# One projection of an attention block as seven products of 2x2 blocks instead of four plain ones

## The chip, the core and the metric

The kernel runs on one core of a Trainium2 chip. The metric is device time in microseconds (us) of one execution, lower is better; the time of a version is the median of several runs. The core has five engines that work side by side and wait for each other by semaphores: PE (TensorE, matmuls, whose weight loads the profile shows apart as PEld), DVE (VectorE), ACT (ScalarE), POOL (GpSimd) and SP (SyncE, used here to issue DMAs). DMAs are issued on the queues of SP, ACT and POOL. Matmuls write to PSUM, eight banks of 128 x 512 floats, which DVE and ACT empty into SBUF.

## The reference

A decoder layer over 512 tokens of 1024 channels, in float32. `h = rms_norm(x)`, then one projection gives the inputs of two attention branches of 8 heads of 64 channels each:

```python
proj = h @ w_in[l]
qa, ka, va, za, qb, kb, vb, zb, gl_a, gl_b = jnp.split(proj, SPLIT_POINTS, axis=-1)
...
oa = moba_attention(qa, ka, split_heads(va, N_HEADS_MOBA), rel_bias)
ob = stick_breaking_attention(split_heads(qb, N_HEADS_SB), split_heads(kb, N_HEADS_SB),
                              split_heads(vb, N_HEADS_SB))
ya = (merge_heads(oa) * jax.nn.silu(za)) @ w_up_moba[l]
yb = (merge_heads(ob) * jax.nn.silu(zb)) @ w_up_sb[l]
y = jax.nn.sigmoid(gl_a + gb[:D_MODEL]) * ya + jax.nn.sigmoid(gl_b + gb[D_MODEL:]) * yb
x = x + y @ w_out[l]
```

The first branch is causal softmax attention with normed q and k and a bias. The second takes `z = q k / 8` and weights each value by sigmoid(z) times the product of the (1 - sigmoid(z)) of the keys between. The change concerns `qb`, 512 tokens by 512 channels.

## The kernel before

**Precision.** Every float32 operand is split into a high part, rounded to the format that PE multiplies, and a low part, the rest. `mm3` (lines 214 to 219) makes one product of three matmuls: high by low, low by high, high by high, added up in PSUM.

**The weights' stream.** All weights lie in one array `w` of blocks of 128 x 1024 floats (512 KB), in the order in which they are used; `_layout` builds it on the host from `FRONT` and `FILLS` (lines 46 to 55). `load_w` (143) hands out the next block and keeps three under way. `fetch_w` (150) brings a block: a DMA on SP's queue into one of three raw tiles (line 162), the high part on ACT (line 171), the low part on DVE (line 173), each into one of three tiles. Blocks that are sums of others skip the DMA on SP: they have been put together in a tile of pool `vp` (eight tiles of 128 x 1024, which also hold the transposed q and k of the first branch for a while and the finished values) by a DMA that loads one block and a DMA that adds another (`accum_op`), both on POOL's queue. `load_v` (107) and `add_v` (114) do that for the values, `sum_w` (130) for the output projection.

**Order.** Tile, the layer under the kernel, orders the instructions of each engine when the program is built and assigns buffers then. `tc.issue_after(ins)` puts an instruction behind another on the same engine.

1. Norm of x, q and k of the first branch, then seven merge gates (`FRONT`).
2. `values()` (644 to 683): va and vb as seven products of 2x2 blocks (the scheme of Strassen in the variant of Winograd). x^T is cut into four blocks of 512 channels by 256 tokens, w likewise. Four sums of blocks of x^T (S1 to S4) are made by `mix_x` (345), four of blocks of w (T1 to T4) by the adding DMAs. `product` (635) multiplies one block of x^T (as PE's weights) by one block of w (128 x 512 moving): 24 matmuls of 128x512 on two weight blocks. The products are added up on the way out of PSUM (lines 657 to 682).
3. Eight pairs of heads, four of each branch (774 to 793). A pair is: `scores` (485), 24 matmuls into six banks with tag `s`; the weighted sum of the pair before the last (`finish`, 768, with `weighted`, 577), into a bank with tag `pj`, emptied by DVE at line 591; then for each head softmax (510) or stick-breaking (526), 32x32 transposes (554), a way through DRAM and back (`put` on SP's queue, `get` on ACT's). PE does not wait for that: `fill()` (756) puts projections between, from the list `FILLS`, one entry of it at each of four places per pair. The entries are `z`, the gates `g`, `q` and `k` of the second branch, and `up`, two products of the branch's output with its up matrix. Each is one block of the weights' stream.

A projection is `chunk_ct` (476): one block of 1024 columns holds the weights of 128 channels; 8 x 3 matmuls with 128x128 of the weights as PE's weights and 128 channels by 512 tokens of x^T moving give 128 channels by 512 tokens in one bank, with tag `pj` (two banks) or `s`. `f_q` (602) scales that by 1/8 and splits it with `split` (401) for `scores`; q has four such entries.

4. The rest of the second branch's up products, and the output projection as seven products of the same kind.

## Time and profile before

| | |
|---|---|
| time, median of 3 runs | 385.66 us (385.57 to 385.77) |
| the profiled execution | 385.91 us, of it 384.1 span of the core |
| matmuls | 1863 |
| DMAs with weights on SP's queue (512 KB) | 58, median 5.4 us from issue to landing |
| DMA packets | 35882, 83.22 MB, 217 GB/s in the mean |

The profile is that of one execution, so sums are made against its 385.91 us. "Busy" of PE counts each matmul from its start to its modelled end, in a pipeline: 389 ns for a matmul of 128x512, though the next one starts earlier. What a matmul costs is therefore read from the distance of starts, which the chain in order of time gives. In rows of groups stands the line, engine, operation, out<-in, shape, count, then busy time in us and mean ns of one, then the idle time of the engine before them and what ended it. In rows of a timeline stand the start and the length in us. Times within the kernel count from the start of the span.

### The profile page before, as it was taken

The numbers are of one execution on the slowest core, as the hardware profiler recorded it, in microseconds if no ns is written. First come the engines' busy times: TensorE is split into PE (matmuls) and PEld (weight loads), VectorE is DVE, ScalarE is ACT, GpSimd is POOL, SyncE is SP. The second block draws the span as 40 slices with busy tenths as digits, with TensorE's granted clock in tenths as the row PEclk, the third lists the DMA queues.
The fourth block names the chain that finished last, engine by engine and source line by source line (L and its number), as shares of the span: only waits on it lengthen the run. The fifth ranks groups of instructions, "written<-read, shape, count | busy, mean of one in ns | idle before, by whom it ended". The sixth has DMA issues, their size and how long they took to land.

```text
span 384.1 us, 5319 instructions
## 1 busy us (share of the span) xinstructions
PE 379.7 (99%) x1863; PEld 306.5 (80%) x1863; DVE 283.3 (74%) x495; ACT 204.4 (53%) x345; POOL 74.7 (19%) x117
## 2 busy tenths in 40 slices
PE   8999999999999999999999999999999999999996
PEld 5888888888888888878787887887878877888885
DVE  4828999934786868696775948939849725999963
ACT  5775657347755747774665428327245222368540
POOL 3859959220100000000000000002000000330310
PEclk9999999999999999999999999999999999999999
DMA  7989798996710567886766485894876851599955
GB/s 272 330 333 336 211 214 287 267 332 216 162 58 3 190 192 254 250 275 163 263 148 232 127 292 188 194 342 135 203 280 185 263 208 56 148 266 297 164 148 181
DMA packets 35882, 83.22 MB, mean 217 GB/s; under 512 B 3848, under 2 KB 16648, under 8 KB 35856
## 3 DMA queue, kind: packets, MB, share of 16 engines
q1 hardware_dynamic: 27840, 53.24, 42.0%
q0 software_dynamic: 5568, 18.90, 20.5%
q10 hardware_dynamic: 2448, 10.75, 8.1%
q8 instruction: 14, 0.23, 0.2%
q14 instruction: 12, 0.10, 0.1%
HBM read 65.03 MB, written 14.70 MB: 208 GB/s over the span
## 4 chain that ended last, share of the span: by engine, by line
PE 99%; DVE 0%; issue 0%
PE gl L217 8%; PE gl L218 8%; PE gl L219 8%; PE poa L586 2%; PE pob L586 2%; PE sa L496 2%; PE sb L496 2%; PE zb L217 2%; PE kb L217 2%; PE qb L217 2%; PE yb L217 2%; PE za L217 2%; PE yb L218 2%; PE ka L218 2%; PE ka L217 2%; PE qb L218 2%
## 5 line engine op out<-in xcount | busy, mean ns | idle before, releaser
L173 DVE TENSOR_TENSOR wl<-wr,wh 128x1024 fp32r<-128x1024 f32 (+1 forms) x62 | 73.2, 1181 | 41.4 <-ACT wh L171 41.3
L171 ACT ACTIVATE wh<-wr 128x1024 fp32r<-128x1024 f32 (+1 forms) x62 | 63.8, 1029 | 42.7 <-PE ya L219 10.8
L217 PE MATMUL gl<-xl,wh 128*128 128x512 f32 x128 | 49.8, 389 | 0.0
L218 PE MATMUL gl<-xh,wl 128*128 128x512 f32 x128 | 49.8, 389 | 0.0
L219 PE MATMUL gl<-xh,wh 128*128 128x512 f32 x128 | 49.8, 389 | 0.0
L132 POOL COPY turn_of<-ptb 1x1 f32<-1x1 f32 x3 | 1.5, 504 | 174.4 <-DMA ptb<-pdb 174.4
L613 ACT ACTIVATE gl<-gl,x 128x512 f32<-128x512 f32 x16 | 11.0, 686 | 37.4 <-PE gl L219 32.9
L219 PEld LDWEIGHTS gl<-xh,wh 128*128 128x128 f32 x128 | 24.0, 188 | 5.0
L217 PEld LDWEIGHTS gl<-xl,wh 128*128 128x128 f32 x128 | 24.0, 188 | 5.0
L218 PEld LDWEIGHTS gl<-xh,wl 128*128 128x128 f32 x128 | 24.0, 188 | 5.0
L516 DVE CUSTOM_DVE_ANT_0 pa<-sa,om 128x512 f32<-128x512 f32 (+3 forms) x32 | 14.2, 482 | 11.0 <-PE sa L496 11.0
L536 DVE TENSOR_TENSOR_SCAN sx<-om,begin 128x512 f32<-128x512 f32 (+1 forms) x16 | 17.0, 1075 | 4.5 <-ACT om L533 4.5
L518 ACT ACTIVATE pa<-pa,m 128x512 f32<-128x512 f32 (+3 forms) x32 | 17.7, 554 | 4.0 <-DVE m L516 3.9
L558 DVE STREAM_TRANSPOSE turnedb<-pb 128x384 f32<-128x384 f32 (+1 forms) x24 | 14.1, 600 | 0.0
L558 DVE STREAM_TRANSPOSE turneda<-pa 128x384 f32<-128x384 f32 (+1 forms) x24 | 14.1, 604 | 0.0
L217 PE MATMUL zb<-xl,wh 128*128 128x512 f32 x32 | 12.8, 400 | 0.0
L217 PE MATMUL kb<-xl,wh 128*128 128x512 f32 x32 | 12.7, 396 | 0.0
L217 PE MATMUL qb<-xl,wh 128*128 128x512 f32 x32 | 12.7, 396 | 0.0
L217 PE MATMUL yb<-olb,wh 128*128 128x512 f32 x32 | 12.6, 393 | 0.0
L217 PE MATMUL za<-xl,wh 128*128 128x512 f32 x32 | 12.6, 393 | 0.0
L218 PE MATMUL zb<-xh,wl 128*128 128x512 f32 x32 | 12.5, 390 | 0.0
L218 PE MATMUL yb<-ohb,wl 128*128 128x512 f32 x32 | 12.5, 390 | 0.0
(385 smaller groups left out, 1022.9 us busy)
## 6 DMA issues: line engine op xcount, KB each, us to landing
wr<-in_w SPq DMA_DIRECT2D x58, 512.0 KB, 5.4
pda<-turneda SPq DMA_DIRECT2D x32, 160.0 KB, 2.9
pta<-pda ACTq DMA_DIRECT2D x8, 640.0 KB, 5.5
pdb<-turnedb SPq DMA_DIRECT2D x32, 160.0 KB, 4.2
ptb<-pdb ACTq DMA_DIRECT2D x8, 640.0 KB, 6.4
xn<-in_x SPq DMA_DIRECT2D x8, 256.0 KB, 6.0
om<-e_dr SPq DMA_DIRECT2D x8, 256.0 KB, 4.7
xr<-in_xT SPq DMA_DIRECT2D x7, 256.0 KB, 5.6
```

The source lines that it names most:

```text
L171: A.activation(hi[:, a:b], raw[:, a:b], AF.Copy)
L173: low[c] = V.tensor_tensor(lo[:, a:b], raw[:, a:b], hi[:, a:b].bitcast(F32), op=ALU.subtract).ins
L217: T.matmul(ps, aH, bL, start=start, stop=False, skip_group_check=on)
L218: T.matmul(ps, aL, bH, start=False, stop=False, skip_group_check=on)
L219: end[0] = T.matmul(ps, aH, bH, start=False, stop=stop, skip_group_check=on).ins
L496: T.matmul(ps[b][:, c:c + n], x[o, i * P:(i + 1) * P], y[o, :n], start=m == 0, stop=m == 2)
L516: V.tensor_tensor_reduce(rows[i], sc[i], bias[:, S - n:], scale=1.0, scalar=3e38, op0=ALU.add, op1=ALU.min, accum_out=m[:, 0, i:i + 1])
L518: A.activation(rows[i], rows[i], AF.Exp, bias=m[:, 0, i:i + 1], scale=-1.0, accum_out=m[:, 1, i:i + 1])
L536: V.tensor_tensor_scan(sx[:, n - 1::-1] if n == S else sx[:, :n][:, ::-1], om[:, S + 1 - n:][:, ::-1], begin[:, S - n:S][:, ::-1], 0.0, op ...
L558: V.transpose(turned[:, :, at:at + n, :].rearrange("p q j r -> p j q r"), rows[i].rearrange("p (j q c) -> p j q c", j=n, q=4))
L586: guard[0] = T.matmul(po[o, :].rearrange("p (a n r) -> p a n r", a=4, r=32)[:, :, i:i + n, :], vv[j][:, c:c + HD], src, start=j == NT - 1, ...
L613: evicted.append(A.activation(g, ps, AF.Sigmoid, bias=mb[:, i:i + 1]).ins)
```

## The change

qb is computed as seven products as well, right behind the values, by `queries()`. There the blocks of w are PE's weights and those of x^T move, so that the result stands in columns (channels by tokens) as `scores` wants it. `product_ct` is such a product: on one weight block, for n of two halves of 128 channels and k of four blocks of 128 input channels, one `mm3` with 128x128 of w and 128 x 256 tokens of x^T, so 24 matmuls of 128x256. The blocks and sums of x^T are those that the values use. The sums of w's blocks are made by the same pair of DMAs on POOL's queue, four of them (T1 to T4), each one tile of 512 KB. Results go to two tiles of pool `vp`; `f_q` then only scales and splits, from SBUF, and takes no weight block.

`FILLS` loses the four weight blocks of q. Its entries per pair hold two blocks in the first pair, three in the second to seventh and four in the eighth (before: three in the first four, four in the others); one more stands behind the pairs in both. The up products take both banks with tag `s` wherever they stand.

```diff
-FILLS = ("q:0", "k:0", "za:0", "",
-         "za:1", "q:1", "g:7", "",
-         "k:1", "za:2", "g:8", "",
-         "q:2", "za:3", "g:9", "",
-         "k:2", "q:3", "zb:0", "g:10",
-         "zb:1", "k:3", "up:0", "g:11",
-         "zb:2", "g:12", "up:1", "g:13",
-         "zb:3", "g:14", "up:2", "up:3",
+FILLS = ("za:0", "k:0 q:0", "", "",
+         "za:1", "g:7 q:1", "k:1", "",
+         "za:2", "g:8", "zb:0", "",
+         "za:3", "k:2 q:2", "g:9", "",
+         "zb:1", "g:10", "k:3 q:3", "",
+         "zb:2", "g:11", "up:0", "",
+         "zb:3", "g:12", "up:1", "",
+         "g:13", "g:14", "up:2", "up:3",
          "g:15")
...
+    ORDER = {"v": ("11", "22", "T2", "21", "T3", "T1", "T4"), "q": ("11", "T1", "21", "T2", "22", "T3", "T4")}
...
     def f_q(p):
-        qb.append(split(chunk_ct(f"qb{p}"), f"qb{p}", HD ** -0.5))
+        qb.append(split(q_raw[p // 2][:, p % 2, :], f"qb{p}", HD ** -0.5))
...
         for t in range(2):
             A.activation(low_b[t], X[t], AF.Copy)
+        summed.append(each(add_sum, "q", ("T1",), each(load_sum, "q", ("T1",), summed[-1])))
         Y = [bank("s", f"vw{t}") for t in range(2)]
         product(Y, s1, True)
...
+        summed.append(each(add_sum, "q", ("T2",), each(load_sum, "q", ("T2",), summed[-1])))
         product(X, a22, False)
...
+    def product_ct(ps, a, start):
+        hi, lo = load_w()
+        for n in range(2):
+            for k in range(4):
+                ks = slice((2 * k + n) * P, (2 * k + n + 1) * P)
+                mm3(ps[:, n * HS:(n + 1) * HS], hi[:, ks], lo[:, ks], *a[k], start and n + k == 0, k == 3, True)
+
+    def queries():
+        q = [wide(f"qb{c}").rearrange("p (n t) -> p n t", n=2) for c in range(2)]
+        q11, q21, q12, q22 = (q[c][:, :, r * HS:(r + 1) * HS] for c in range(2) for r in range(2))
...
+        X, D, Z, Y, E = (bank("s", f"q{n}") for n in "xdzye")
+        product_ct(X, a11, True)
+        A.activation(q11, cols(X), AF.Copy)
+        product_ct(D, s1, True)
+        A.activation(q22, cols(D), AF.Copy)
+        summed.append(each(add_sum, "q", ("T3",), each(load_sum, "q", ("T3",), summed[-1])))
+        product_ct(Z, a12, True)
+        V.tensor_tensor(q11, cols(Z), q11, op=ALU.add)
+        product_ct(X, s2, False)
+        V.tensor_tensor(q12, q22, cols(X), op=ALU.subtract)
+        each(add_sum, "q", ("T4",), summed[-1])
+        product_ct(Y, s4, True)
+        V.tensor_tensor(q12, cols(Y), q12, op=ALU.add)
+        product_ct(X, s3, False)
+        V.tensor_tensor(q22, q22, cols(X), op=ALU.subtract)
+        A.activation(q21, cols(X), AF.Copy)
+        product_ct(E, a22, True)
+        V.tensor_tensor(q21, cols(E), q21, op=ALU.add)
+        return q
+
+    q_raw = queries()
...
         for kind, i in fills.pop(0):
+            home[0] = "s" if kind == "up" else tag
             make[kind](i)
```

`load_sum` and `add_sum` are `load_v` and `add_v` with the kind (values or q) as an argument. On the host, `_layout` cuts the columns of q into four blocks ahead of the fills instead of four blocks of 128 channels among them; the bytes are the same.

## The prediction, made before the result was known

> **What bounds the kernel now.** I read the page first (busy time, then the chain that ended last), the chain in order of time, the busy time of each engine by stage, and last the single instructions of DVE, POOL and PE where the change lies. The page and the head of its chain:

> ```profile
> span 384.1 us, 5319 instructions
> ...
> PE 379.7 (99%) x1863; PEld 306.5 (80%) x1863; DVE 283.3 (74%) x495; ACT 204.4 (53%) x345; POOL 74.7 (19%) x117
> ...
> PE 99%; DVE 0%; issue 0%
> ```

> TensorE is never let go: what is taken from its work comes off the time, as long as nobody makes it wait. The chain in order of time gives the starts of the eight pairs of heads:

> ```profile
> 126.03 2.07 PE sa L496 x24
> ...
> 144.63 2.07 PE sa L496 x24
> ...
> 163.23 2.07 PE sa L496 x24
> ...
> 184.15 2.07 PE sa L496 x24
> ...
> 205.07 2.07 PE sb L496 x24
> ...
> 231.43 2.07 PE sb L496 x24
> ...
> 257.79 2.07 PE sb L496 x24
> ...
> 284.15 2.07 PE sb L496 x24
> ```

> A pair is its scores (2.07), from the third pair on the weighted sum of two pairs before, and its projections. The stages, with length and busy time of PE, PEld, DVE, ACT, POOL, then clock, DMA share and GB/s:

> ```profile
> 57.00:88.00 31.00, 31.00 (x138) 25.68 (x137) 21.63 (x40) 14.73 (x22) 14.05 (x16) 1.00 0.97 301
> 88.00:126.00 38.00, 38.00 (x170) 31.20 (x168) 26.53 (x30) 24.93 (x33) 1.79 (x2) 1.00 0.37 106
> 126.03:144.63 18.60, 18.60 (x98) 15.30 (x98) 13.97 (x39) 11.79 (x24) 0.00 (x0) 1.00 0.62 185
> ...
> 184.15:205.07 20.92, 20.92 (x118) 16.57 (x118) 15.19 (x41) 12.41 (x25) 0.00 (x0) 1.00 0.69 222
> 205.07:231.43 26.36, 26.36 (x142) 21.08 (x142) 18.68 (x27) 12.24 (x21) 0.00 (x0) 1.00 0.60 205
> 231.43:257.79 26.36, 26.36 (x142) 21.07 (x142) 21.43 (x29) 11.66 (x20) 1.60 (x3) 1.00 0.76 227
> ```

> PE fills every stage, even the one from 57 to 88 us in which the DMA engines are busy 0.97 of the time.

> **The change, part by part.** *Removed:* four projections of q, 24 matmuls of 128x512 each. A pair with four projections lasts 26.36, one with three 20.92: a projection costs 5.44 us of PE, and four cost 21.8. The values confirm the step: 168 matmuls of 128x512 are their 7 products, in 38.0 us, 0.226 us each.

> *Added:* seven products of 2 x 4 x 3 = 24 matmuls, 168 in all, each with 256 moving columns and a fresh 128x128 block of weights. The trace has that form in the last product, in the chain in order of time:

> ```profile
> 376.44 0.12 PE ox L217
> ...
> 377.88 0.23 PE ox L217
> ...
> 379.26 0.12 PE ox L217
> ```

> Between the first two rows lie 12 matmuls of 128x256: 1.44 us, 0.120 each. Between the last two, 6 of 128x512: 1.38 us, 0.230, slower than the 0.226 of the values. Scaled by 0.226/0.230 the step is 0.118, which I take: 168 of them are 19.8 us. The bounds are 0.120 (20.2) and half of 0.226 (19.0). So PE has 21.8 - 19.8 = 1.9 us less to do (rounded from 21.76 and 19.82), between 1.6 and 2.8.

> For the weights, this is the row of a load:

> ```profile
> L218 PEld LDWEIGHTS qb<-xh,wl 128*128 128x128 f32 x32 | 6.0, 188 | 1.2
> ...
> L217 PEld LDWEIGHTS ox<-wl,yh 128*128 128x128 f32 x16 | 3.0, 189 | 0.5
> ```

> A load takes 188 ns from start to end, the matmuls of the last product follow each other at 120: loads overlap the matmuls and each other there, so 72 more loads cost nothing beyond the step. [...]

> *Weight splits.* Seven blocks of 1024 columns in place of four: three more times ACT L171 and DVE L173. The products also empty PSUM with three copies and six sums where q had none; the split of each q head pair stays, now from SBUF.

> ```profile
> L173 DVE TENSOR_TENSOR wl<-wr,wh 128x1024 fp32r<-128x1024 f32 (+1 forms) x62 | 73.2, 1181 | 41.4 <-ACT wh L171 41.3
> L171 ACT ACTIVATE wh<-wr 128x1024 fp32r<-128x1024 f32 (+1 forms) x62 | 63.8, 1029 | 42.7 <-PE ya L219 10.8
> ```

> and from the groups of the values' stage:

> ```profile
> L668 DVE TENSOR_TENSOR vas<-vz,vas 128x512 f32<-128x512 f32 x2 | 1.4, 686 | 0.6 <-PE vz L219 0.6
> ...
> L673 ACT ACTIVATE vc<-vx 128x512 f32<-128x512 f32 x2 | 1.2, 598 | 1.1 <-PE vx L219 1.1
> ```

> In the 19.8 us of the new stage DVE has 7 x 1.18 + 6 x 0.69 = 12.4, ACT 7 x 1.03 + 3 x 0.60 = 9.0. A block lasts PE 24 x 0.118 = 2.83 us there and 38.0/14 = 2.71 in the values, which run without a gap at the same work per block. I cost it at nothing; the cover is 7 us of free DVE.

> *The sums of q's blocks* (three loads and four adding DMAs of 512 KB on POOL's queue) stand behind v's last adding DMA. Each waits for the one it builds on, and POOL waits with it; nothing else is on POOL until the fifth pair. ACT waits for a sum at its split, and behind that wait stand the splits of the next blocks and the copies out of PSUM, so a late sum stops PE.

> ```profile
> 99.01 0.90 POOL L121 DMA_DIRECT2D vT2b<-in_w  x1 [0.84 <-DVE wl L173]
> ...
> 105.40 1.23 DVE L173 TENSOR_TENSOR wl<-vT3a,wh 128x1024 fp32r<-128x1024 f32 x1
> ...
> 111.33 1.22 DVE L173 TENSOR_TENSOR wl<-vT1a,wh 128x1024 fp32r<-128x1024 f32 x1
> ```

> ```profile
> DMA to landing us min/median/max: 5.7/8.7/12.2
> ```

> ```profile
> DMA to landing us min/median/max: 5.1/7.3/10.0
> ```

> The last two rows are v's loads (L112) and v's adding DMAs (L121). Of the eight tiles of that pool six hold v's sums at 100 us and one the values' first half, so one is free: I start the first load at 99.9. With median landings (8.7, 7.3): T1 is loaded at 108.6 and summed at 115.9; T2's load takes the tile that T3a leaves at 106.6, is issued at 109.5 and lands at 118.2, its sum at 125.5; T3 lands at 127.8, its sum at 135.1. The blocks come on PE at 126.0 + 2.83 n: T1 at 128.9, T2 at 134.5, T3 at 140.2, T4 at 143.0. A split needs 2.2 us before that: 126.7, 132.3, 138.0, 140.8. T4 is added into T2's tile after T2's split, which starts when PE leaves the third block before it, at 128.9, and ends at 131.1; it lands at 138.4. The margins are 10.8, 6.8, 2.9 and 2.4 us: no wait.

> *The pairs.* They hold two projections in the first, three in the next six and four in the last. The first lasts 2.07 + 2 x 5.5 = 13 us. The next pair's scores need the banks of its scores, last read here 9.1 us after the start of the pair:

> ```profile
> 134.86 0.28 DVE L516 CUSTOM_DVE_ANT_0 pa<-sa,om 128x128 f32<-128x128 f32 x1
> ```

> That leaves 4 us. The pairs of the second branch fall from 26.36 to 20.9. The fifth keeps three weight splits and the evictions of z, k and q, 18.7 us of DVE (its row above); the sixth loses two splits and one eviction of k, 21.4 - 2 x 1.18 - 0.68 = 18.4. DVE is then busy nine tenths of the pair, ACT under two thirds. The DMA share rises to at most 0.76 x 26.36 / 20.92 = 0.96 with nothing taken off, the share at which the stage from 57 us kept PE full. The tight place is the bank of the weighted sum, which the second projection of a pair takes over:

> ```profile
> 209.38 0.50 PE L217 MATMUL kb<-xl,wh 128*128 128x512 f32 x1
> ...
> 213.78 0.68 DVE L591 TENSOR_TENSOR oa<-poa,za 128x512 f32<-128x512 f32 x1
> ...
> 214.95 0.39 PE L217 MATMUL qb<-xl,wh 128*128 128x512 f32 x1
> ...
> 239.76 0.68 DVE L591 TENSOR_TENSOR oa<-poa,za 128x512 f32<-128x512 f32 x1
> ...
> 265.59 0.68 DVE L591 TENSOR_TENSOR ob<-pob,zb 128x512 f32<-128x512 f32 x1
> ...
> 292.41 0.68 DVE L591 TENSOR_TENSOR ob<-pob,zb 128x512 f32<-128x512 f32 x1
> ```

> L591 frees it 0.5 us before the second projection in the fifth pair; at the same 9.9 us after the start the margin is 0.9 in the sixth, 1.4 in the seventh and 0.9 in the eighth. I leave it at nothing, since before L591 DVE has the same stick-breaking work as now. The up products move into the scores' banks, straight ahead of the next scores in the sixth and seventh pair: their second eviction (0.69, the form of L668) has until the third group of scores, two thirds into the 2.07, so 0.7 us to spare; nothing too.

> The sum against the profiled execution: 385.91 - 1.9 = 384.0, its span 384.1 - 1.9 = 382.2. The median of the runs is 385.66, 0.25 below that execution, so the forecast is 383.8, with a range of its own from 383.0 (2.7 off) to 384.5 (0.7 of stalls).

> **The rivals.** *A, the late bank.* One weight split more ahead of L591 (1.2 us) in the fifth to eighth pair makes PE wait 0.7, 0.3, 0 and 0.3. That is 1.3: 385.1. For it: the 0.5 us of margin and DVE at nine tenths. Against: there are fewer splits per pair.

> *B, the sums come late, and the kernel is slower.* If the free tile goes to another use, the first load waits for T3a's tile at 106.6, 6.7 us later, and T3's sum passes its 2.9 us of margin by 3.8: PE waits 3.8, the net is +1.9, 387.6. It decides from a start at 102.8 on; every us beyond costs one, and from 104.7 the gain is gone. The longest landings (12.2 and 10.0) would do the same from 99.9. Against it: in this stage the DMA share is 0.37, and the two adding DMAs issued in it at 97.3 and 99.0 landed in 5.1 and 5.9, below the medians I used:

> ```profile
> vT2a<-in_w POOLq DMA_DIRECT2D x1, 512.0 KB, 5.1
> vT2b<-in_w POOLq DMA_DIRECT2D x1, 512.0 KB, 5.9
> ```

> *C, weight loads not hidden:* 72 more at 188 ns are 13.5, less 1.9: 397.3. For it speaks only that a load is longer than the step of 128x256; the 24 matmuls of the last product speak against it.

> **How the numbers follow.** A measurement of this kernel can tell about 0.2%, 0.8 us: faster is below 384.9, slower above 386.4. Forecast 0.66; A 0.17, of which a third falls below 384.9; B 0.14; C 0.03. So faster is 0.66 + 0.05 = 0.71, the same 0.12, slower 0.17. The range goes from the forecast's lower bound, 383.0, over A to 386.0, where a second split stands ahead of L591 in one of those pairs (0.9 more); B and C, 0.17, are left out.

> **What would show it.** Right: the new stage of 168 matmuls lasts 19.8 us at 0.118 each without a gap; the pairs start 13.0, 18.6 and then 20.9 apart; PE's share stays at 99%; ACT's splits of q's four sums wait for PE, not for a DMA. Wrong: a step near 0.13 or more, which takes all of the gain; ACT or POOL waiting for the sums of T2, T3 or T4 with a gap on PE behind it; a gap of PE ahead of the second projection of a pair or of the scores, ended by DVE L591 or L711; pairs of 22 us and more, which would make DVE the bound there.

## The result, and the profile after

The changed kernel takes 389.1 us (median of 6 runs, 387.68 to 389.66), the kernel before 385.7 (6 runs beside them, 385.54 to 385.98): a ratio of 1.0084, with a 95% interval of 1.0067 to 1.0100. The forecast was 383.8, with a range of 383.0 to 386.0. It was wrong, and on the wrong side. The profiled execution of the changed kernel took 388.84 us, 387.1 of it span. The ratios, here and below, leave out an execution more than 1.5% above the fastest of its kernel; that is one, the slowest of kernel 1 below.

The page of the changed kernel, its span, PE's busy time and the chain that ended last by engine:

```profile
span 387.1 us, 5491 instructions
...
PE 379.2 (98%) x1935; PEld 309.3 (80%) x1935; DVE 290.3 (75%) x503; ACT 209.0 (54%) x351; POOL 79.4 (21%) x124
...
PE 95%; DVE 2%; DMA 1%; issue 1%; ACT 0%; DVEq 0%; ACTq 0%
```

PE held 99% of the chain before; now it waits somewhere. The starts of the eight pairs in the chain in order of time show where:

```profile
145.53 2.05 PE sa L504 x24
...
158.68 2.07 PE sa L504 x24
...
177.28 2.07 PE sa L504 x24
...
198.20 2.07 PE sa L504 x24
...
219.12 0.91 PE sb L504 x5
...
245.19 2.07 PE sb L504 x24
...
266.11 2.07 PE sb L504 x24
...
287.02 2.07 PE sb L504 x24
```

The pairs last 13.15, 18.6, 20.92, 20.92, **26.07**, 20.92 and 20.91. All but the fifth are as forecast. Stretches of the changed kernel (length, busy time of PE, PEld, DVE, ACT, POOL, then clock, DMA share, GB/s): the stage of q with the last matmul of the values and the step to the scores, the fourth pair, the wait in the fifth, the matmuls behind it, the sixth pair:

```profile
125.22:145.47 20.25, 20.25 (x171) 20.11 (x169) 11.00 (x11) 9.24 (x11) 2.27 (x3) 1.00 0.62 167
198.20:219.12 20.92, 20.92 (x118) 16.57 (x118) 15.31 (x43) 11.99 (x25) 0.00 (x0) 1.00 0.88 283
...
229.00:232.60 3.60, 0.46 (x2) 0.14 (x1) 3.60 (x6) 2.88 (x4) 0.00 (x0) 1.00 0.73 200
232.60:239.58 6.98, 6.92 (x23) 5.64 (x24) 5.45 (x9) 0.00 (x0) 0.00 (x0) 0.76 0.29 65
245.19:266.11 20.92, 20.92 (x118) 16.57 (x118) 19.92 (x28) 11.48 (x20) 1.76 (x3) 1.00 0.72 214
```

The seven products of q fill PE without a gap. The waits of PE, and its timeline at the fifth pair's second projection, the gate g:10:

```profile
PE gl L226 <- DVE wl L181: 3.2, 1, 3.2
```

```profile
229.00 0.46 PE L225 MATMUL gl<-xl,wh 128*128 128x512 f32 x1
232.66 0.80 PE L226 MATMUL gl<-xh,wl 128*128 128x512 f32 x1 [3.20 <-DVE wl L181]
233.25 0.63 PE L227 MATMUL gl<-xh,wh 128*128 128x512 f32 x1
...
235.81 0.52 PE L227 MATMUL gl<-xh,wh 128*128 128x512 f32 x1
236.16 0.39 PE L225 MATMUL gl<-xl,wh 128*128 128x512 f32 x1
```

The first matmul goes, the second waits for the low half of its weights: 3.66 from start to start in place of 0.23, a loss of 3.4 us. The next eight steps are 0.59, six of 0.43 and 0.35 in place of 0.226, with the granted clock at 0.76 over the stretch: another 1.7. Behind them the step is 0.23 again. The projection takes 10.58 us (229.00 to 239.58) in place of 5.44, so 5.1 are lost in one place. The rest of the span: the stage of q is 1.5 shorter than four projections (20.25 against 21.76), and this execution opened 0.65 faster; 5.1 - 1.5 - 0.65 = 3.0, which is 387.1 - 384.1.

Why the low half is late stands in the timelines of ACT, DVE and SP's DMA queue:

```profile
214.21 0.62 ACT L412 ACTIVATE qb2h<-qb 128x512 fp32r<-128x512 f32 x1
219.16 0.69 ACT L621 ACTIVATE gl<-gl,x 128x512 f32<-128x512 f32 x1 [4.32 <-PE gl L227]
...
227.00 1.06 ACT L179 ACTIVATE wh<-wr 128x1024 fp32r<-128x1024 f32 x1
```

```profile
214.96 0.68 DVE L413 SCALAR_TENSOR_TENSOR qb2l<-qb,qb2h 128x512 fp32r<-128x512 f32 x1
220.68 1.22 DVE L544 TENSOR_TENSOR_SCAN sx<-om,begin 128x512 f32<-128x512 f32 x1 [5.04 <-ACT om L541]
...
230.08 0.94 DVE L554 TENSOR_TENSOR_SCAN sx<-om_short,begin 128x386 f32<-128x386 f32 x1
...
231.38 1.22 DVE L181 TENSOR_TENSOR wl<-wr,wh 128x1024 fp32r<-128x1024 f32 x1
```

```profile
207.05 4.80 SPq L573 DMA_DIRECT2D pda<-turneda  x8
211.95 1.81 SPq L170 DMA_DIRECT2D wr<-in_w  x3
```

ACT and DVE both stand idle from 215 or 216 to 219 or 220 us. The split of g:10 could go there, but in their fixed order it comes after the stick-breaking of the fifth pair, on DVE after the scans of both heads. Its load is among the three that SP issues from 211.95, behind the eight puts of the fourth pair, which wait for DVE's transposes; the load is in the tile about 5 us later.

### The profile page after: what moved, and what is told of

The parts are those of the page before. It is cut to its first block, busy times and chain, and to the rows that moved or that the text cites. A ratio compares the mean times of both kernels' runs of the same rounds, so it can differ in the third digit from the quotient of the medians.

```text
span 387.1 us, 5491 instructions
## 1 busy us (share of the span) xinstructions
PE 379.2 (98%) x1935; PEld 309.3 (80%) x1935; DVE 290.3 (75%) x503; ACT 209.0 (54%) x351; POOL 79.4 (21%) x124
## 4 chain that ended last, share of the span: by engine, by line
PE 95%; DVE 2%; DMA 1%; issue 1%; ACT 0%; DVEq 0%; ACTq 0%
PE gl L226 8%; PE gl L227 8%; PE gl L225 8%; PE pob L594 2%; PE sa L504 2%; PE za L225 2%; PE yb L225 2%; PE yb L226 2%; PE ka L225 2%; PE za L226 2%; PE yb L227 2%; PE ya L226 2%; PE za L227 2%; PE vx L227 2%; PE ka L227 2%; PE kb L227 2%
## 5 line engine op out<-in xcount | busy, mean ns | idle before, releaser
L181 DVE TENSOR_TENSOR wl<-wr,wh 128x1024 fp32r<-128x1024 f32 (+1 forms) x61 | 71.7, 1179 | 31.8 <-ACT wh L179 31.4
L179 ACT ACTIVATE wh<-wr 128x1024 fp32r<-128x1024 f32 (+1 forms) x61 | 62.7, 1028 | 45.0 <-PE ya L227 12.0
L226 PE MATMUL gl<-xh,wl 128*128 128x512 f32 x128 | 50.7, 396 | 3.2 <-DVE wl L181 3.2
L621 ACT ACTIVATE gl<-gl,x 128x512 f32<-128x512 f32 x16 | 11.0, 687 | 30.4 <-PE gl L227 29.6
L526 ACT ACTIVATE pa<-pa,m 128x512 f32<-128x512 f32 (+3 forms) x32 | 17.6, 552 | 1.5 <-DVE m L524 1.3
L524 DVE CUSTOM_DVE_ANT_0 pa<-sa,om 128x512 f32<-128x512 f32 (+3 forms) x32 | 13.5, 484 | 0.0
L226 PE MATMUL za<-xh,wl 128*128 128x512 f32 x32 | 12.5, 390 | 0.0
L226 PE MATMUL ka<-wh,xl 128*128 128x512 f32 x32 | 12.5, 390 | 0.0
## 6 DMA issues: line engine op xcount, KB each, us to landing
wr<-in_w SPq DMA_DIRECT2D x57, 512.0 KB, 5.3
qT<-in_w POOLq DMA_DIRECT2D x6, 512.0 KB, 6.3
```

The source lines that it names most:

```text
L179: A.activation(hi[:, a:b], raw[:, a:b], AF.Copy)
L181: low[c] = V.tensor_tensor(lo[:, a:b], raw[:, a:b], hi[:, a:b].bitcast(F32), op=ALU.subtract).ins
L226: T.matmul(ps, aL, bH, start=False, stop=False, skip_group_check=on)
L524: V.tensor_tensor_reduce(rows[i], sc[i], bias[:, S - n:], scale=1.0, scalar=3e38, op0=ALU.add, op1=ALU.min, accum_out=m[:, 0, i:i + 1])
L526: A.activation(rows[i], rows[i], AF.Exp, bias=m[:, 0, i:i + 1], scale=-1.0, accum_out=m[:, 1, i:i + 1])
L621: evicted.append(A.activation(g, ps, AF.Sigmoid, bias=mb[:, i:i + 1]).ins)
```

## The experiments

**Theories.** T: the whole loss is that one split, standing behind the stick-breaking because its load stands behind puts; without it the time is about 384. D: DVE is the bound of a pair that has stick-breaking and only three projections; taking this wait away only moves it to the next place, and less than half comes back. Blocks are counted by their place in the weights' stream: g:10 is item 48, k:3 behind it 49.

**1. Three loads ahead of the puts.** SP issues the loads of items 46 to 48 ahead of the fourth pair's puts.

```diff
+        if m == 3:
+            for c in (46, 47, 48):
+                load_early(c)
...
+            with tc.issue_after(before_put[0]) if before_put[0] and (br, h) == ("a", 6) else nullcontext():
                 nc.sync.dma_start(bass.AP(tensor=dr.tensor, offset=dr.offset + a * PQ,
```

> The raw loads of stream items 46, 47 and 48 (the fifth pair's second and third projections among them) are issued on SP ahead of the puts of the fourth pair; nothing else is changed. Theory T (one misplaced split): the weights of g:10 are then split in the idle time that ACT and DVE have in the trace at 215 to 220 us, ahead of the fifth pair's stick-breaking; the 3.2 us wait of PE in front of its second matmul and the slow clock behind it (1.7 us) both go, the fifth pair lasts 20.9 instead of 26.1, and the time is 389.1 - 5.1 = 384.0, faster than the kernel before by about 0.4%. Theory D (DVE is the bound of a pair with three projections): the wait only moves to the next split or to the eviction of the weighted sum; less than half comes back, above 386.5.

Measured 385.31 (11 runs, 384.47 to 390.58), ratio 1.0001 (0.9978 to 1.0024). The fifth pair lasts 20.92. But the executions lie far apart: seven between 384.47 and 385.33, four between 387.15 and 390.58. The profiled one is the slowest of them, with other waits:

```profile
PE ox L237 <- DVE wl L187: 2.1, 1, 2.1
PE zb L237 <- ACT gl L634: 1.3, 1, 1.3
```

The first place is as T says; the waits that came up elsewhere are of the kind that D says. What the other slow executions waited for is not shown. The edit did more than it was meant to: with the loads earlier, the order of ACT and DVE came out otherwise in later pairs too.

**2. The split ahead by force.** The load stays; the fifth pair's first head, and the weighted sum in that pair, wait for the split.

```diff
...
+            first = br == "b" and h == 0
+            with tc.issue_after(high[count[0] - 1]) if first else nullcontext():
+                with tc.issue_after(low[count[0] - 1]) if first else nullcontext():
+                    rows = (softmax if br == "a" else stick)(h, sc[h], bias)
...
```

> The load stays where it is, behind the puts; instead the stick-breaking of the fifth pair's first head is issued on ACT and DVE behind the split of item 48, which waits for its load until about 217 us. T: PE's wait at the second matmul of g:10 goes, as with the load moved, but the stick-breaking of the first head starts some 1 to 2 us later, which is hidden if nothing waits for it: 384.0 to 385.5. D: the wait moves to the stick-breaking's readers or to the next split; above 386.5.

Measured 390.91 (390.05 to 391.66), ratio 1.0132 (1.0114 to 1.0150). The fifth pair lasts 20.92, but the sixth 0.8 and the seventh 5.4 more than that; in the seventh ACT's split waits 2.4 us for a load that again stands behind puts. T's figure failed; D was right for this edit.

**3. The wait filled with matmuls.**

```diff
+        if name == "gl10":
+            with tc.issue_after(end[0]):
+                for _ in range(14):
+                    T.matmul(ps, xH[0][:, :P], xH[0], start=True, stop=True)
```

> 14 matmuls of 128x512 without use (x by x, 14 x 0.226 = 3.2 us) stand on PE in the place of the wait ahead of g:10, into g:10's own bank; the split is as late as before. T with the lowered clock as a consequence of the wait: the granted clock stays at 1.00 in that chunk and its 23 other matmuls go at 0.226, so 1.7 us come back: 387.4. If the low clock has another cause than the idle PE: 389.1 still. If the dummies were in the way (the wait was not a wait for weights): 389.1 + 3.2 = 392.3.

Measured 388.44 (388.05 to 388.78), ratio 1.0068 (1.0054 to 1.0082). The stretch of the 14 and g:10, by the same columns as above:

```profile
229.48:238.50 9.02, 8.97 (x39) 7.06 (x39) 9.02 (x13) 2.89 (x4) 0.00 (x0) 1.00 0.58 175
```

It is 1.56 us shorter than in the changed kernel, at a clock of 1.00: the low clock came from the wait. T's 387.4 was missed by one us, which was lost again in the scores of the seventh pair; they waited 0.2 us for the eviction of an up product and took 3.0 in place of 2.07.

**4. Two and four projections.** `FILLS` with two entries beside the first four pairs and four beside the next three. It is the order of the kernel before with q taken out and the fifth pair filled up, not that kernel's own.

```diff
+         "za:1", "k:1 q:1", "", "",
+         "za:2", "g:7", "", "",
+         "za:3", "k:2 q:2", "", "",
+         "zb:0", "zb:1", "k:3 q:3", "g:8",
```

> q of the second branch in seven products as in the changed kernel, but the projections beside the pairs as in the kernel before: two in most pairs of the first branch, four in those of the second. T: what costs is only the place of one split, not the products of q; with four projections beside the fifth pair its third one may wait for its split behind the stick-breaking, but the pair has 5.4 us more of PE work to cover it: no wait or one below 1 us, 384.0 to 385.0. D: DVE has room in pairs of 26.4 us, so also about 384. [...]

Measured 398.57 (397.95 to 398.92), ratio 1.0329 (1.0315 to 1.0343). All theories missed. The products of q run as before, so they are not the cause. The fifth pair takes 38.0 us where 26.4 were due, the fourth 17.6 where 15.3 were. PE waits for the way through DRAM, for ACT and for DVE:

```profile
PE kb L225 <- ACT wh L179: 2.9, 1, 2.9
PE poa L594 <- DMA pta<-pda: 2.9, 1, 2.9
PE kb L226 <- DVE wl L181: 1.3, 2, 0.9
```

The first of these is again a weight load behind puts: it goes out on SP at 221.97, behind sixteen puts issued from 199.08 on. The second is the get of the softmax's result from DRAM; that pairs of 15 us are too short for it is likely, and not shown by itself.

**5. The puts on POOL's queue.**

```diff
-            nc.sync.dma_start(bass.AP(tensor=dr.tensor, offset=dr.offset + a * PQ,
+            (nc.gpsimd if (br, h) >= ('a', 6) else nc.sync).dma_start(bass.AP(tensor=dr.tensor, offset=dr.offset + a * PQ,
```

> The puts of the rows of weights (L573) go from POOL's queue in place of SP's, from the fourth pair on; nothing else is edited, so on SP no weight load stands behind a put any more, in any pair. In the fixed order the splits of items 48 and 49 then stand ahead of the fifth pair's scans. Theory T, in its wider form (a split is late where its load stands on SP behind puts that wait for DVE's transposes): all pairs from the third to the seventh last 20.9, no wait and no slow clock, 384.0 in every execution. Theory D (DVE is the bound of a pair with three projections, a wait only moves on): a wait of 1 to 3 us in one of the pairs five to seven, 386 or more. Third: POOL is slow with the puts (32 of them at 0.6 to 0.9 us each by its own DMAs, some of them behind the sums of the output's blocks): the gets come late, ACT waits for them, 388 or more.

Measured 388.23 (386.68 to 389.81), ratio 1.0053 (1.0034 to 1.0072). g:10 does not wait, but two others do, the second with a low clock behind it; the fifth pair is 1.3 too long, the eighth 3.9:

```profile
PE gl L225 <- DVE ob L599: 2.1, 1, 2.1
PE kb L225 <- DVE zb L608: 1.0, 1, 1.0
```

The wait of the fifth pair is as D expected; splits and evictions changed places on DVE here, too. The larger one, in the eighth pair, is as the third view has it: ACT's get there waits for a put on POOL, and the pair's scans behind that get:

```profile
287.93 0.60 ACT L541 ACTIVATE om<-sb 128x512 f32<-128x512 f32 x1 [7.63 <-DMA pdb<-turnedb]
```

That is 3.9 us after the start of the pair, against 1.1 in the changed kernel. The last put had left POOL at 285.5, five us after DVE's last transpose for it.

**6. The first edit, and a get later.** In its profile ACT's get of the sixth pair's second head held the eviction of a gate.

```diff
+                with tc.issue_after(evicted[-1]) if m in (4, 5, 6) else nullcontext():
+                    done[m, 1] = get(*head(m, 1), done[m, 1])
```

> As the kernel with the three loads ahead of the fourth pair's puts, and besides ACT issues the get of a pair's second head (L580) behind the eviction of the gate (L621) in the fifth to seventh pair. In the profiled execution of the former this get, waiting for its put, held that eviction until 266.5 and PE for 1.3 us at the next pair's first projection; executions between 384.5 and 390.6 followed. T with this as the second place: the executions close up at 384.0 to 385.3 and none is above 386. D: another wait takes its place, executions stay spread, median above 385.5. The late adding DMA at the end (a wait of 2.1 us in front of the last product there) can still come up in single executions.

Measured 386.57 (12 runs, 384.38 to 389.83), ratio 1.0031 (1.0001 to 1.0061). The executions did not close up; the profiled one (388.66) waits 1.3 us for the eviction of an up product in the eighth pair, a low clock follows, and 3.8 us are lost from that pair on. Against T. What decides in a single execution of this kernel and of the first whether such a wait comes up was not found.

**7. The same fault put into the kernel before.** The split of the fifth pair's second projection (q of the fourth head pair), its high half on ACT and its low half on DVE, is moved behind the scans.

```diff
+            if c == 42:
+                late[c] = hi, lo, raw
+                continue
...
+            rows = (softmax if br == "a" else stick)(h, sc[h], bias)
+            if (br, h) == ("b", 1):
+                split_late(42)
```

> The kernel before, unchanged but for one thing: the weight split of the fifth pair's second projection (q of the fourth head pair) is issued behind the scans of that pair's second head, where the changed kernel has its own. T: the same loss as in the changed kernel, a wait of about 3.4 us at the second matmul of that projection and about 1.7 us of lowered clock, 385.7 + 5.1 = 390.8. D: a pair with four projections has DVE time to spare, so that work waits less; and if the loss were due to the products of q or to three projections, nothing changes: 385.7 to 387.

Measured 392.91 (392.09 to 393.04), ratio 1.0181 (1.0168 to 1.0194): 7.2 us lost. The fifth pair, and PE in it:

```profile
204.73:237.48 32.75, 29.45 (x141) 22.56 (x140) 19.95 (x27) 12.20 (x21) 0.74 (x2) 0.90 0.56 176
```

```profile
217.00 0.80 PE L227 MATMUL qb<-xl,wh 128*128 128x512 f32 x1 [2.15 <-ACT wh L183]
217.59 0.63 PE L227 MATMUL zb<-xl,wh 128*128 128x512 f32 x1
...
220.22 0.80 PE L228 MATMUL qb<-xh,wl 128*128 128x512 f32 x1 [1.14 <-DVE wl L184]
```

32.75 in place of 26.36: 3.3 of waits, the rest low clock. T had 390.8, 2.1 too little: here the high half is late as well, so PE waits twice. With it a few splits and evictions of later pairs changed places, but the sixth and seventh pair last 26.36 and 26.42, within 0.1 of before. One split in that place costs the old kernel as much, and more, with four projections in the pair and four plain ones of q. Neither the products of q nor three projections per pair are needed for the loss.

**8. One instruction left out.** ACT, POOL and SP keep the order of the changed kernel; on DVE a few instructions of the fifth pair change places.

```diff
+            if c == 48:
+                lo = None
+                continue
...
+            mm3(ps, hi[:, ks], lo[:, ks] if lo is not None else xL[0][:, :P], xH[k], xL[k], k == 0, k == KT - 1)
```

> The changed kernel with one instruction left out: DVE's low half of the weights of item 48 (g:10). PE loads a tile of x in its place, the same number of matmuls; every other instruction stays in the order of the changed kernel on every engine. Theory T (the loss is this one split, the rest of the change does what was forecast): 389.1 - 5.1 = 384.0, all pairs from the third on 20.9. Theory D (DVE is the bound of these pairs): a wait of 1 to 3 us comes up in another place behind it, 386 or more.

Measured 385.33 (10 runs, 385.25 to 386.02), ratio 0.9986 (0.9975 to 0.9997): 3.8 of the 5.1 came back, where T had all of them, and the executions lie close together. The fifth pair lasts 22.00, 1.1 more than the others, with one wait at k:3 for the bank that z leaves; behind the longer wait of the changed kernel it had not shown:

```profile
PE kb L228 <- DVE zb L611: 0.7, 1, 0.7
```

**9. Twelve low halves left out**, items 46 to 57, in the same manner. On ACT a get and two high halves also change places.

> As the former, with the low halves of items 46 to 57 left out, all weight splits of DVE for the fifth to eighth pair: 12 x 1.18 = 14 us of DVE's work in some 84 us. T: the same as with the one left out, 384.0, since nothing else waited. D: if the former still has a wait or a spread of its executions over 1 us, this one has none, 383.9 to 384.2; if this one has it too, the cause is neither DVE's work nor the one split, but a DMA (the gets, or the adding loads at the end).

Measured 384.65 (384.34 to 385.02), ratio 0.9973 (0.9963 to 0.9984). No wait on DVE is left; the fifth pair is 0.4 too long. Fourteen us off DVE bring only 0.7 beyond the one instruction: most of the loss hangs on where that one stands, little on how much DVE has to do.

**10. Seven low halves on POOL**, on top of edit 6.

```diff
-                low[c] = V.tensor_tensor(lo[:, a:b], raw[:, a:b], hi[:, a:b].bitcast(F32), op=ALU.subtract).ins
+                low[c] = (G if c in (47, 49, 50, 52, 53, 55, 56) else V).tensor_tensor(lo[:, a:b], raw[:, a:b], hi[:, a:b].bitcast(F32), op=ALU.subtract).ins
```

> The whole computation again: the kernel with the three loads ahead and the get behind the gate's eviction, and besides the low halves of seven weight blocks (items 47, 49, 50, 52, 53, 55, 56) computed by POOL in place of DVE. T: no different from its base, whose best executions are at 384.4 to 384.9. D (what spreads that kernel from 384.4 to 389.8 is DVE's lateness with the evictions, 1.3 us at the up product's in its profile): 8 us less on DVE, executions close up at 384.0 to 385.0, median below 385, faster than the kernel before. If POOL's subtraction is slower than about 4 us, or stands behind the waits of the adding DMAs on POOL, PE waits for it: 387 or more.

Measured 395.79 (394.43 to 396.61), ratio 1.0250 (1.0230 to 1.0269). POOL takes 2.68 us for one (mean of 7), within the 4 allowed, and yet PE waits 3.5 us for DVE in the fifth pair, and 1.4 twice more further on; what DVE's rows were like beside POOL's is in the last section.

**11. One load on POOL's queue.** After edit 8 the remedy is to bring the load of item 48 alone forward.

```diff
-                    nc.sync.dma_start(raw[:, a:b], src[:, a:b])
+                    (nc.gpsimd if c in (48,) else nc.sync).dma_start(raw[:, a:b], src[:, a:b])
```

> The changed kernel with one DMA moved: the load of the weights of item 48 (g:10) goes from POOL's queue, which is empty then, in place of SP's, where it stands behind the puts of the fourth pair. Nothing is left out. Its split then stands in the idle time of ACT and DVE ahead of the fifth pair's scans; the other splits stay behind them. Theory T: the wait in g:10 goes as with the low half left out; what is left is the small wait for the bank of z at k's projection (0.7 us and its slow clock there): 385.0 to 385.5, and 384.2 if DVE, with one split less behind the scans, is in time for it. Theory D (a wait moves on whenever work is moved ahead of the scans): above 386.5, as with the loads ahead of the puts or the puts on POOL, whose executions spread from 384.4 to 390.

Measured 385.18 (11 runs, 384.91 to 385.84), ratio 0.9988 (0.9980 to 0.9997), with the whole computation. The load goes out at 199.05, the low half is made in DVE's idle time, and the small wait at k:3 is left (0.8 us). The orders of ACT and DVE came out a little otherwise behind it here, too, but no wait came of that.

**12. And z ahead of the transposes.**

```diff
+            with tc.issue_after(z_out[0]) if b and m in (4,) else nullcontext():
+                turned = turn(br, h, rows)
```

> As the former, and besides DVE evicts z of the fifth pair (L608) ahead of the transposes of that pair's second head, so that the bank for k's projection is free about 3 us earlier. T: the last wait of that pair goes, all pairs 20.9: 384.2 (the forecast of 383.8 and 0.4 for the step of 0.120 in place of 0.118 in the stage of q), faster than the kernel before by 0.4%. D: no better than the former.

Measured 384.37 (5 runs, 383.97 to 384.58), ratio 0.9964 (0.9950 to 0.9977): faster than both kernels, and 0.2 from the figure that T gave. DVE's timeline and the pairs' starts in the chain:

```profile
215.44 1.23 DVE L181 TENSOR_TENSOR wl<-wr,wh 128x1024 fp32r<-128x1024 f32 x1 [0.26 <-ACT wh L179]
...
220.82 1.23 DVE L544 TENSOR_TENSOR_SCAN sx<-om,begin 128x512 f32<-128x512 f32 x1 [3.56 <-ACT om L541]
...
233.72 0.69 DVE L608 TENSOR_TENSOR zb<-zb,zb 128x512 f32<-128x512 f32 x1
```

```profile
219.26 2.07 PE sb L504 x24
...
240.22 2.07 PE sb L504 x24
```

The low half of g:10 stands at 215.44 ahead of the scans, z's eviction at 233.72 in time for k:3 at 234.6, and the fifth pair lasts 20.96.

**What the twelve decide.** T is shown, by taking the one instruction away (8), by putting the fault into the old kernel (7) and by moving one load (11), with z's eviction for the small wait behind it (12). Its "whole loss" was a little too much: 3.8 of 5.1 came back with the one, most of the rest with z. D as a bound is refuted: in kernel 12 DVE does the same work and no pair waits. What D described is real in another sense: edits 1, 2, 5, 6 and 10 changed the order or the lengths of more instructions than the one, and waits came up in other places whose margins are small.

## Why the prediction was wrong, point by point

- *Removed, 21.8 us*: right. The pairs start 13.15, 18.6 and 20.92 apart.
- *Added, 19.8 us at 0.118*: the step is 0.120, the bound that stood in the row of the last product; six products take 17.28 (125.22 to 142.50), and the stage 20.25 to the scores. To scale it by 0.226/0.230 had no ground: six matmuls of 128x512 straight ahead of the first of those rows, from 375.08 on, came at 0.227. That term was mis-sized by 0.4: without any wait the forecast should have been 384.2, and kernel 12 has 384.37.
- *Loads hidden* (against rival C): right. A load lasts 192 ns in the new stage and a step 0.120. So loads overlap the matmuls and each other here as in the last product (188 against 120); what lets them, no run here shows.
- *Splits and evictions in the new stage at nothing*: right; DVE is busy 11.0 of 20.25, ACT 9.2.
- *Sums on POOL, margins 10.8 to 2.4 us*: no wait of PE, so rival B did not happen. But T2's load went out at 112.3, not 109.5, and T3's at 125.4, not 119.1, since each waited for a tile. ACT's splits of T3 and T4 did wait for a DMA, 3.62 us (the row below) and 1.95, where the prediction had them wait for PE alone. Their low halves were done at 138.76 and 141.67, one us ahead of the matmuls that read them: of 2.9 and 2.4 us of margin one was left, and that PE did not wait was partly luck.

```profile
136.34 1.06 ACT L179 ACTIVATE wh<-qT 128x1024 fp32r<-128x1024 f32 x1 [3.62 <-DMA qT<-in_w]
```

- ***The pairs, "I leave it at nothing": the step that failed.*** It added up DVE's busy time (18.7 of 20.9) and checked when the bank of the second projection comes free (L591). It did not ask when that projection's weights come: where their split stands in the order of ACT and DVE, and behind what their load stands on SP's queue. In the kernel before the low half of the fifth pair's second projection is done at 202.5, four us ahead of the first scan; only the third one's stands among the scans, and PE needs that later. With one block less per pair the stream slid by a place against the puts, so that now the second projection's load goes out behind the fourth pair's puts.
- *Rival A* named the right pair and the right projection, with another cause (L591, and 0.7 us); the bank did come free late, at 228.84, but 0.16 ahead of the projection. In the sixth to eighth pair of the changed kernel there is no wait, as forecast. The 0.7 us to spare at the up products' bank was as small as said: edits 3, 6 and 10 ran into it. DVE's busy time in the sixth pair, put at 18.4, came to 19.92, and PE did not wait for it.
- *The price of a wait* was taken as its length. A wait with a low clock behind it cost up to 1.7 us more (last section).
- The list of what would show it wrong came near: it had a gap at the second projection, but ended by L591, and pairs of 22 us and more, but as a sign that DVE is the bound; a late weight split was not on it. The chance for all rivals that end slower, 0.17, was too small for a part in which only sums of busy time stood.

## What to carry to other kernels

When work is taken off the engine that bounds a kernel, ask of every operand that it reads afterwards when it will be ready: follow it through each queue with a fixed order, and name what stands ahead of it there, waits included. Free time on an engine is no margin if the piece that is needed first stands last. And cure a misplaced instruction by moving as little else as can be; here the edits that laid more of the order out anew brought their own waits.

## What the runs showed of the hardware that was not expected

```profile
229.23:232.64 3.41, 0.23 (x1) 0.00 (x0) 3.41 (x6) 2.65 (x4) 0.00 (x0) 1.00 0.72 188
232.65:236.06 3.41, 3.40 (x8) 2.76 (x9) 3.41 (x6) 0.00 (x0) 0.00 (x0) 0.50 0.11 30
236.07:239.48 3.41, 3.41 (x16) 2.80 (x16) 1.98 (x3) 0.00 (x0) 0.00 (x0) 1.00 0.44 94
```

Kernel 6, such a stretch and the next, then kernel 10, the same:

```profile
283.23:286.64 3.41, 1.89 (x16) 1.23 (x16) 3.41 (x5) 1.85 (x4) 0.00 (x0) 1.00 0.98 348
286.64:290.05 3.41, 3.41 (x23) 2.38 (x23) 3.31 (x5) 0.87 (x2) 0.00 (x0) 0.50 0.85 221
```

```profile
256.02:259.43 3.41, 2.02 (x9) 1.39 (x9) 3.41 (x5) 1.71 (x4) 0.56 (x1) 1.00 0.49 166
259.43:262.84 3.41, 3.41 (x17) 2.83 (x16) 3.41 (x6) 1.61 (x3) 1.77 (x2) 1.00 0.96 197
```

Counted in such stretches, ten at full clock ahead of these kernels' last matmuls hold 1.52 us of idle PE or more (3.41 - 1.89 = 1.52 in kernel 6, 3.41 - 0.23 = 3.18 in the changed kernel), and each is followed by one at half the clock; none with 1.39 or less is (3.41 - 2.02 in kernel 10). The stretch at half clock cost 1.7 us in the changed kernel, half its length. In kernels 4 and 7 the next one was at half clock as well, after 1.35 and 1.23 us of idle PE in the first. That is what was counted in these runs; why it is so they do not show.

**DVE's rows while POOL subtracts.** Kernel 10, POOL (two subtractions in one row) and DVE in the fifth pair, first a multiply and a scan with POOL idle, then the same two while POOL works:

```profile
229.35 5.55 POOL L187 TENSOR_TENSOR wl<-wr,wh 128x1024 fp32r<-128x1024 f32 x2 [14.93 <-ACT wh L185]
```

```profile
223.14 0.69 DVE L558 TENSOR_TENSOR pb<-pb,sx 128x512 f32<-128x512 f32 x1
223.75 0.95 DVE L556 TENSOR_TENSOR_SCAN sx<-om,begin 128x384 f32<-128x384 f32 x1
...
230.25 2.41 DVE L558 TENSOR_TENSOR pb<-pb,sx 128x512 f32<-128x512 f32 x1
232.58 3.14 DVE L556 TENSOR_TENSOR_SCAN sx<-om,begin 128x384 f32<-128x384 f32 x1
```

0.69 became 2.41, and 0.95 became 3.14: POOL's two last from 229.35 to 234.90, and DVE's two, begun in that time, end at 232.66 and 235.72. They took 3.91 us longer, where two such subtractions on DVE take 2.4 (1.18 each in this kernel). So in these rows the work given to POOL was not taken off DVE; what made DVE's rows longer is not shown.
